# Tiles of 384 rows in a ring of four, and a last store in three pieces, in a grouped softmax

## The chip, the cores and the metric

One core of a Trainium2 chip. The metric is the device time of one execution in microseconds (us). A difference under 2% counts as "same", whatever its sign, so this case is about the sign and the size inside those 2%.

Where the text speaks of single DMA packets, it means the packet records of the trace: start, length, size and queue of each packet that a DMA engine moved. They carry no engine number. A DMA of 128 partitions also leaves 16 records of 4 B (688 for the 43 loads of the changed kernel), and the three pieces of its last store leave 16, 14 and 8. I read them as one per engine that took part, left when that engine is done, and call them end records.

## The reference

```python
B, N, D, G = 4, 4096, 4352, 8          # x: float32
x_g = x.reshape(B, N, G, D // G)
x_g = x_g - x_g.max(axis=-1, keepdims=True)
exp = np.exp(x_g)
out = exp / exp.sum(axis=-1, keepdims=True)
```

16384 rows, each with eight softmaxes over 544 numbers. 285.2 MB come in and 285.2 MB go out.

## The kernel before

A tile is 256 rows, two per partition (`R = 2`), in a ring of six buffers (`NT = 6`). SyncE issues loads, VectorE takes maxima, reciprocals and scales, ScalarE takes the exponentials and issues the stores. A store trails by two tiles and is issued as soon as a new tile has been seen.

```python
R = 2; NT = 6; S = R * NT; LAG = 2
...
def vector_max(n):
    s = n % S
    if s % R == 0:
        take(nc.vector, landed[s // R], 16)
        nc.vector.sem_inc(seen, 1)
    nc.vector.reduce_max(out=mx[:, s, :], in_=row(s), axis=X, negate=True).then_inc(max_done, 1)
...
def store(b, target):
    take(nc.scalar, scaled, R)
    nc.scalar.dma_start(out=target, in_=bufs[b][:, :]).then_inc(stored[b], 16)

def scalar_tile(j, *targets):
    take(nc.scalar, seen)
    for r in range(R):
        if r < len(targets):
            store((j - LAG + r) % NT, targets[r])
        scalar_exp(j * R + r)
...
scalar_tile(nt - 2, ot[nt - 4])
scalar_tile(nt - 1, ot[nt - 3], ot[nt - 2])
store((nt - 1) % NT, ot[nt - 1])           # the last store: one DMA of 128 partitions
...
def vector_rows(lo, hi):
    for n in range(lo, hi):
        vector_max(n + 1)
        vector_scale(n)
```

## Time and profile before

| | before |
|---|---|
| median time, 3 runs | 1330.36 us (1330.23 to 1330.4) |
| span | 1328.5 us |
| VectorE busy / ScalarE busy | 1041.7 / 764.5 us |
| the two DMA queues together | 99.5% of 16 engines' span |
| last store done on 13 engines / two more / the last one | 1319.9 to 1320.3 / 1322.4 / 1326.3 us |

Read it from the bottom: the DMA engines are always busy, so only the edges of the run can be won. The lines are in the prediction. The columns are the stretch in us, its length, the busy time of VectorE, ScalarE and GpSimd (with the number of instructions), the clock, the DMA share and GB/s. A packet counts, whole, in the stretch in which it starts, so a short stretch can be off by one round of packets, and a share can pass 1.

```profile
66.00:82.00 16.00, 15.70 (x21) 11.44 (x32) 0.00 (x0) 1.00 0.97 418
82.00:100.00 18.00, 17.70 (x21) 13.44 (x38) 0.00 (x0) 1.00 1.00 433
1294.00:1309.00 15.00, 6.72 (x17) 5.55 (x16) 0.00 (x0) 1.00 1.03 446
1310.00:1319.80 9.80, 0.00 (x0) 0.00 (x0) 0.00 (x0) 1.00 0.93 401
1320.40:1326.30 5.90, 0.00 (x0) 0.00 (x0) 0.00 (x0) 1.00 0.08 35
```

The reader is to see a full rate up to 1320 and then 6 us in which one slow engine works off its lag.

### The profile page before, as it was taken

The page shows a single profiled execution, that of the slowest core. Times are in us where ns is not written, and L with a number is a line of the kernel's source. Part 1 is how long each engine was busy: PE and PEld are TensorE (multiplying, and loading weights), DVE is VectorE, ACT ScalarE, POOL GpSimd, SP SyncE. Part 2 cuts the span into 40 slices and gives each one's busy share as a digit, 9 for nine tenths or more (in the row PEclk, how much of TensorE's full clock was granted, in tenths as well). Part 3 has the DMA queues.
Part 4 walks back from the last instruction along what each step waited for, and adds up shares of the span by engine and source line. Part 5 has one row for each costly group of instructions (what it writes and reads, how often), then busy time and mean ns, then how long its engine had stood idle before and what let it go on. Part 6 is the DMA issues. An engine that isn't in the chain of part 4 may idle for free. (4 is left out here: it accounts for less than half of the span.)

```text
span 1328.5 us, 4328 instructions
## 1 busy us (share of the span) xinstructions
DVE 1041.7 (78%) x1280; ACT 764.5 (58%) x2049; POOL 0.2 (0%) x4
## 2 busy tenths in 40 slices
DVE  5899987887877878778787787877878778787781
ACT  3677755655556556565565655655556555565551
POOL 0000000000000000000000000000000000000000
DMA  9999999999999999999999999999999999999997
GB/s 403 418 436 435 434 433 429 432 435 436 435 433 428 432 435 436 435 434 430 429 436 435 435 434 433 426 436 436 434 434 433 427 435 436 435 434 433 427 433 328
DMA packets 18439, 570.49 MB, mean 429 GB/s; under 512 B 2048, under 2 KB 2048, under 8 KB 2048
## 3 DMA queue, kind: packets, MB, share of 16 engines
q1 hardware_dynamic: 9216, 285.22, 49.8%
q10 hardware_dynamic: 9216, 285.22, 49.7%
q14 instruction: 7, 0.06, 0.0%
HBM read 285.21 MB, written 285.21 MB: 429 GB/s over the span
## 5 line engine op out<-in xcount | busy, mean ns | idle before, releaser
L88 ACT ACTIVATE xt<-xt,mx 128x544 f32<-128x544 f32 x1024 | 751.3, 735 | 534.1 <-ACTq L59 534.1
L70 DVE TENSOR_REDUCE mx<-xt 128x8 f32<-128x4352 f32 x128 | 599.2, 4682 | 238.3 <-DVEq L59 235.3
L79 DVE TENSOR_SCALAR xt<-xt,rs 128x544 f32<-128x544 f32 x1024 | 434.2, 498 | 19.2
L88 ACT ACTIVATION_READ_ACCUMULATOR xt<-xt,mx 128x1 f32 x1024 | 192.0, 187 | 0.0
L75 DVE RECIPROCAL rs<-sm 128x8 f32<-128x8 f32 x128 | 24.8, 193 | 4.2 <-DVEq L59 4.2
L120 ACT ACT_TABLE_LOAD x1 | 1.3, 1283 | 0.9 <-SPq L47 0.9
L156 POOL MEMSET const-bfloat16-1.0<- 128x1 bf16 x1 | 0.1, 103 | 0.0
L156 POOL MEMSET const-uint8-127<- 128x1 uint8 x1 | 0.1, 102 | 0.0
L156 POOL MEMSET const-float32-0.0<- 128x1 f32 x1 | 0.1, 100 | 0.2 <-issue 0.2
L156 POOL MEMSET const-float32-1.0<- 128x1 f32 x1 | 0.1, 99 | 0.0
## 6 DMA issues: line engine op xcount, KB each, us to landing
xt<-in_x_dram SPq DMA_DIRECT2D x64, 4352.0 KB, 30.5
out_dram<-xt ACTq DMA_DIRECT2D x64, 4352.0 KB, 51.3
```

Source lines behind the costliest of these rows:

```text
L70: nc.vector.reduce_max(out=mx[:, s, :], in_=row(s), axis=X, negate=True).then_inc(max_done, 1)
L75: nc.vector.reciprocal(out=rs[:, s, :], in_=sm[:, s, :]).then_inc(rec_done, 1)
L79: i = nc.vector.tensor_scalar_mul(out=xr[:, g, :], in0=xr[:, g, :], scalar1=rs[:, s, g:g + 1])
L88: i = nc.scalar.activation(out=xr[:, g, :], in_=xr[:, g, :], func=Exp, bias=mx[:, s, g:g + 1], scale=1.0, accum_out=sm[:, s, g:g + 1],)
L120: nc.scalar.preload_act_table(Exp)
L156: nc = _bacc.Bacc("TRN2", target_bir_lowering=False, num_devices=1)
```

## The change

The intent: fewer and longer packets (three rows per partition in place of two), the same 12 rows in SBUF, and at the end less work for two of the engines (4 packets in place of 8), so that a slow one among them no longer ends alone. The `seen` semaphore goes: the store of tile j-1 now comes after the exponential of tile j's first row.

```diff
-    R = 2
-    NT = 6
+    R = 3
+    NT = 4
     ...
-    def scalar_tile(j, *targets):
-        take(nc.scalar, seen)
-        for r in range(R):
-            if r < len(targets):
-                store((j - LAG + r) % NT, targets[r])
-            scalar_exp(j * R + r)
+    def scalar_tile(j, target):
+        scalar_exp(j * R)
+        take(nc.scalar, scaled, R)
+        nc.scalar.dma_start(out=target, in_=tile_of(j - 1)).then_inc(stored[(j - 1) % NT], 16)
+        for n in range(j * R + 1, min((j + 1) * R, nr)):
+            scalar_exp(n)
     ...                                   # 42 tiles of 384 rows, one of 256
-    store((nt - 1) % NT, ot[nt - 1])
+    take(nc.scalar, scaled, last_rows)
+    for lo, hi in ((0, 64), (64, 120), (120, P)):
+        nc.scalar.dma_start(
+            out=ot_last[lo:hi, :], in_=tile_of(last)[lo:hi, :]).then_inc(stored[last % NT], 16)
```

More of the change, by code (lines that the diff above doesn't have):

```diff
@@ L19 @@
     P = 128
-    R = 2
-    NT = 6
+    R = 3
+    NT = 4
     S = R * NT
-    LAG = 2
     xf = x.flatten_outer_dims()
@@ L27 @@
     Dg = D // G
-    nt = N // (P * R)
-    turns = (nt - LAG) // NT
-    rest = LAG + turns * NT
-    assert rest == nt - 2
+    nr = N // P
+    last = (nr - 1) // R
+    last_rows = nr - last * R
+    nt = last + 1
+    turns = (last - 1) // NT
     f32 = mybir.dt.float32
@@ L34 @@
     Exp = mybir.ActivationFunctionType.Exp
-    xt = xf.rearrange("(t p r) d -> t p (r d)", p=P, r=R)
-    ot = of.rearrange("(t p r) d -> t p (r d)", p=P, r=R)
-    turn_out = of[:turns * S * P, :].rearrange("(u b p r) d -> u b p (r d)", b=NT, p=P, r=R)
+    xt = xf[:last * P * R, :].rearrange("(t p r) d -> t p (r d)", p=P, r=R)
+    ot = of[:last * P * R, :].rearrange("(t p r) d -> t p (r d)", p=P, r=R)
+    turn_out = of[:turns * P * S, :].rearrange("(u b p r) d -> u b p (r d)", b=NT, p=P, r=R)
+    xt_last = xf[last * P * R:, :].rearrange("(p r) d -> p (r d)", p=P)
+    ot_last = of[last * P * R:, :].rearrange("(p r) d -> p (r d)", p=P)
     landed = [tc.alloc_semaphore(f"landed{b}") for b in range(NT)]
     stored = [tc.alloc_semaphore(f"stored{b}") for b in range(NT)]
-    seen = tc.alloc_semaphore("seen")
     max_done = tc.alloc_semaphore("max_done")
@@ L59, in take, with tile_of @@
         engine.sem_inc(sem, -n).wait_op(sem, n, "sem-ge")
+    def tile_of(t):
+        return bufs[t % NT][:, :(R if t < last else last_rows) * D]
     def row(s):
@@ L68, in vector_max @@
             take(nc.vector, landed[s // R], 16)
-            nc.vector.sem_inc(seen, 1)
         nc.vector.reduce_max(out=mx[:, s, :], in_=row(s), axis=X, negate=True).then_inc(max_done, 1)
@@ L96, in scalar_exp @@
         i.then_inc(exp_done, 1)
-    def store(b, target):
+    def scalar_tile(j, target):
+        scalar_exp(j * R)
         take(nc.scalar, scaled, R)
-        nc.scalar.dma_start(out=target, in_=bufs[b][:, :]).then_inc(stored[b], 16)
-    def scalar_tile(j, *targets):
-        take(nc.scalar, seen)
-        for r in range(R):
-            if r < len(targets):
-                store((j - LAG + r) % NT, targets[r])
-            scalar_exp(j * R + r)
+        nc.scalar.dma_start(out=target, in_=tile_of(j - 1)).then_inc(stored[(j - 1) % NT], 16)
+        for n in range(j * R + 1, min((j + 1) * R, nr)):
+            scalar_exp(n)
     for t in range(nt):
@@ L114 @@
             nc.sync.wait_ge(stored[b], 16 * (t // NT))
-        nc.sync.dma_start(out=bufs[b][:, :], in_=xt[t]).then_inc(landed[b], 16)
+        nc.sync.dma_start(
+            out=tile_of(t), in_=xt[t] if t < last else xt_last).then_inc(landed[b], 16)
     for b in range(NT):
-        nc.sync.wait_ge(stored[b], 16 * ((nt - b + NT - 1) // NT))
+        parts = 2 if b == last % NT else 0
+        nc.sync.wait_ge(stored[b], 16 * ((nt - b + NT - 1) // NT + parts))
     nc.scalar.preload_act_table(Exp)
-    for j in range(LAG):
-        scalar_tile(j)
+    for n in range(R):
+        scalar_exp(n)
     with loop(nc.scalar) as u:
         for b in range(NT):
-            scalar_tile(LAG + b, turn_out[u, b])
-    scalar_tile(nt - 2, ot[nt - 4])
-    scalar_tile(nt - 1, ot[nt - 3], ot[nt - 2])
-    store((nt - 1) % NT, ot[nt - 1])
+            scalar_tile(b + 1, turn_out[u, b])
+    for j in range(turns * NT + 1, nt):
+        scalar_tile(j, ot[j - 1])
+    take(nc.scalar, scaled, last_rows)
+    for lo, hi in ((0, 64), (64, 120), (120, P)):
+        nc.scalar.dma_start(
+            out=ot_last[lo:hi, :], in_=tile_of(last)[lo:hi, :]).then_inc(stored[last % NT], 16)
     def vector_rows(lo, hi):
@@ L136 @@
     vector_max(0)
-    vector_rows(0, LAG * R)
+    vector_rows(0, R)
     with loop(nc.vector):
-        vector_rows(LAG * R, LAG * R + S)
-    vector_rows(rest * R, nt * R - 1)
-    vector_scale(nt * R - 1)
+        vector_rows(R, R + S)
+    vector_rows(R + turns * S, nr - 1)
+    vector_scale(nr - 1)
 _INS = ['x']
```

## The prediction

> **What bounds the kernel now.** I read, in this order: the page's bars by slice and DMA rows (which resource is full), the issues with their times to landing, the DMA queue's own waits, the engines' groups, and last the timeline where the loads end.
>
> ```profile
> DVE 1041.7 (78%) x1280; ACT 764.5 (58%) x2049; POOL 0.2 (0%) x4
> ...
> DMA  9999999999999999999999999999999999999997
> GB/s 403 418 436 435 434 433 429 432 435 436 435 433 428 432 435 436 435 434 430 429 436 435 435 434 433 426 436 436 434 434 433 427 435 436 435 434 433 427 433 328
> DMA packets 18439, 570.49 MB, mean 429 GB/s; under 512 B 2048, under 2 KB 2048, under 8 KB 2048
> ...
> q1 hardware_dynamic: 9216, 285.22, 49.8%
> q10 hardware_dynamic: 9216, 285.22, 49.7%
> ...
> xt<-in_x_dram SPq DMA_DIRECT2D x64, 4352.0 KB, 30.5
> out_dram<-xt ACTq DMA_DIRECT2D x64, 4352.0 KB, 51.3
> ```
>
> The two DMA queues together fill 99.5% of 16 engines for the whole span. VectorE is idle 22% of it, ScalarE 42%. So bytes bound the kernel: 570.4 MB near 434 GB/s. Three slices are lower: the first two (403, 418) and the last (328). Those edges are all that this change can win or lose; between them the rate is flat. One load takes 30.5 us to land and one store 51.3 us, although a tile's share of the time is 1328.5/64 = 20.8 us: both queues always have work waiting.
>
> ```profile
> SPq L115 <- DMA out_dram<-xt: 1225.8, 58, 73.6
> SPq L117 <- DMA out_dram<-xt: 77.2, 1, 77.2
> ```
>
> The loader waits only for stores to leave a buffer; it never makes the DMA engines wait while stores are queued.
>
> ```profile
> 48.61 5.47 ACTq L100 DMA_DIRECT2D out_dram<-xt  x1
> ...
> 56.38 4.68 DVE L70 TENSOR_REDUCE mx<-xt 128x8 f32<-128x4352 f32 x1 [3.05 <-issue]
> ...
> 63.08 0.34 ACTq L100 DMA_DIRECT2D out_dram<-xt  x1
> ```
>
> The first store is issued at 48.61, its issue takes 5.47 us (later ones 0.34), and VectorE loses 3.05 us as it enters its loop.
>
> ```profile
> 1280.54 4.69 DVE L70 TENSOR_REDUCE mx<-xt 128x8 f32<-128x4352 f32 x1 [4.08 <-DVEq L59]
> 1280.63 0.35 ACTq L100 DMA_DIRECT2D out_dram<-xt  x1
> ...
> 1288.98 0.34 ACTq L100 DMA_DIRECT2D out_dram<-xt  x1
> ...
> 1303.55 0.34 ACTq L100 DMA_DIRECT2D out_dram<-xt  x1
> ```
>
> The last tile lands just before 1280.54, and one store goes out with it, one at 1288.98, the last at 1303.55. With the ends of stores below, the DMA engines are never empty here.
>
> The trace's single DMA packet records (start, length, size, queue; no engine number) give the rest. A row pair of 34816 B is one packet: 1.288 us long, the next starts 1.2847 us after it. With both queues full the packets alternate one by one. Each DMA ends in 16 records of 4 B, one per engine: so I can see when each engine finishes a tile. In the last store they come at 1319.8 to 1320.3 for 13 engines, 1322.4 for two, and **1326.3 for one**. That one falls back evenly, by some 0.1 us per tile; for the last load it was at 1279.8 where most were at 1273.6. The span ends at 1328.5 and the time is 1330.4, so time = last DMA record + 4.1 us.
>
> [...] 64, 56 and 8 partitions then give 16, 14 and 8 engines with 4, 4 and 1 partitions each. The trace agrees for 128 partitions: 9216 packets a queue = 64 x (128 + 16). [...] The trace shows one slow engine but not its number. [...]
>
> **The change part by part.** The arithmetic per row is unchanged, and so are the bytes and the ring (12 rows). It has four parts.
>
> (a) Fewer, longer packets. Before: 128 x 8 = 1024 packets per engine x 1.2847 = 1315.5, plus 128 end records x 6 ns = 0.8: 1316.3 us. It starts at 1.9, and 1.7 are lost at the two cold starts (first packets of about 2 us in place of 1.288, once for loads and once for stores): 1319.9, as measured. [...] 84 x 8 = 672 x 1.9247 = 1293.4; the small tile 16 x 1.2847 = 20.6; 86 end records 0.5: 1314.5. **-1.8 us.**
>
> (b) The uneven last store. [...] The end moves from 6.3 above the level to 1.3: **-5.0 us.**
>
> (c) The start. Tile 0 lands after 8 x 1.925 + 1.9 + 0.9 = 18.2 us (before: 13.3). Per row VectorE needs 4.6 + 0.35 + 3.3 = 8.25 us, as the rows of the timeline are spaced. Max of row 0 runs 18.9 to 23.5, its exp to 29.5, scale to 33.5; row 1's scale ends at 41.7, max of row 3 at 46.3, its exp at 52.4. Store 0 then goes out at 52.5 and its first packet, as before 9.3 us later, at 61.8. The loads alone last to about 64.4, so nothing is empty yet. Loads, store 0 and its cold start end at 1.9 + 0.9 + 61.6 + 15.4 + 1.0 = 80.8. Store 1 needs three more rows and the exp of row 6: with the 5.5 us of the first issue and the 3 us loop entry, issue at 80 to 81.5, first packet 1.3 later. Load 4 waits for store 0 on its slowest engine and starts about 83. A hole of 0.5 to 2.5: **+1.5 us.**
>
> (d) The end. The new order stores tile j-1 only after the exp of the first row of tile j. At the last tile that is landing L + 0.7 (semaphore) + 4.6 (max) + 6.1 (exp) + 1.4 (issue to packet) = L + 12.8 us; before, a store went out with the landing itself. Without a hole the level would end at 1314.5 + 1.9 + 1.7 + 1.5 = 1319.6, and stores 41 and 42 are 15.4 + 10.3 of it: all else is moved at 1293.9. When is L? Before, loads held 30.5 of about 124 us of a buffer's round, 3 of 12 rows, and 9 rows were left to store when they ended: (1320 - 1273.6)/5.14 = 9.0. The last ring holds 11 rows, so 8 are left: 8 x 5.14 = 41 us before 1319.6, 1278.5 on most engines; the slow one is 4.2 (if it loses per packet) to 6.3 (per byte) later. L = 1283 to 1285, store 41's packets 1295.5 to 1297.6, a hole of 1.6 to 3.7: **+2.7 us.** The slow engine has no hole, which only hides part of its own lag.
>
> Sum: -1.8 - 5.0 + 1.5 + 2.7 = -2.6 us, against 1330.4: **1328.0 us**, -0.2%.
>
> **The rivals.** *The ring starves in every turn.* Store j-1 waits for tile j, and there are only 4 buffers. If each tile lost 1 us, 42 us would be added, 1372. Against: a round is 4 x 30.8 = 123 us and needs load 30.8, landing 0.7, next landing plus max and exp 43, issue 1.3, store 30.8, release and new load 1.9: 108.5. Slack 14.7 us per round, more than the 6 us lag. VectorE needs 24.8 us per tile of 30.8. *All the gain goes to the end.* If one row more is on its way in when loads end, L comes 5 us later and the hole is 7 to 8: 1332 to 1333. For: the balance is set in the first 100 us, which I can't know to a row. [...] Then it keeps its lag and perhaps a ninth packet: level + 4.2 to 7.6, 1328 to 1332; the two 2 us late ones show that lags differ. *The intent comes true without holes:* 1323.6. *Longer packets move at another rate:* 1% would be 13 us; [...] nothing seen speaks for loss.
>
> **Range and chances.** Holes of 0 to 4 at the start and 0 to 7 at the end, and the balance of (b) by 2 either way, give 1324 to 1332. 2% are 26.6 us, four times everything at stake at the edges: faster 0.5%, slower 1.5% (starving ring, longer packets), within 98%.
>
> **What would show each step.** (a) In the DMA view 6192 packets on the load queue and 6214 on the store queue (43 x 16 end records, the last store 16+14+8), the mid-span rate still 433 to 436 GB/s. (b) The last end records lie within about 3 us of each other for the engines with 8 and 9 packets, the slow one among or before them. (c) First store issue near 52.5, second near 81, a slice with a slight dip there. (d) Second-to-last store 11 to 12 us after the last landing, and a drop in the DMA share just then, near 1295. The prediction is wrong if the flat part dips in every tile, if the DMA issues show landings near 16 us (an empty partner queue), or if one engine still ends 6 us alone.

## The result, and the profile after

| | before | changed |
|---|---|---|
| median of 4 runs | 1330.3 us | 1344.42 us |
| lowest to highest | 1329.79 to 1330.4 | 1342.36 to 1352.57 |
| span of the profiled run | 1328.5 us | 1343.3 us |

The ratio is 1.0118, with a 95% interval of 1.0076 to 1.016. Here and below a ratio is the mean time of one kernel's fast runs over that of the other's in the same rounds, so it is not quite the ratio of the medians. That counts as "same" by the 2% line, but the interval is clear of 1: the changed kernel is slower, by 14 us, and 1344.4 lies outside the predicted 1324 to 1332.

From the page of the changed kernel, the rows of rate and packets:

```profile
GB/s 407 412 418 431 434 432 435 432 439 432 428 440 429 437 429 440 431 435 435 428 440 428 439 431 439 432 429 439 429 439 429 440 429 439 432 428 440 428 367 206
DMA packets 12413, 570.49 MB, mean 425 GB/s; under 512 B 1398, under 2 KB 1398, under 8 KB 1398
q10 hardware_dynamic: 6214, 285.22, 49.9%
q1 hardware_dynamic: 6192, 285.22, 49.3%
```

The flat part is as flat as before, the packet counts are the predicted 6192 and 6214, and both queues still look full, 99.2% together. The loss stands in the last two slices, 367 and 206 GB/s. That the queues are "busy" there while the rate is half is what has to be explained. The stretches around the end, same columns as above:

```profile
66.00:82.00 16.00, 15.70 (x21) 11.51 (x31) 0.00 (x0) 1.00 0.99 428
82.00:100.00 18.00, 17.70 (x21) 12.34 (x34) 0.00 (x0) 1.00 0.99 389
1284.00:1294.00 10.00, 8.83 (x11) 5.96 (x16) 0.00 (x0) 1.00 0.99 427
1294.50:1300.00 5.50, 5.35 (x11) 4.50 (x13) 0.00 (x0) 1.00 0.07 28
1300.00:1313.00 13.00, 10.12 (x18) 7.43 (x21) 0.00 (x0) 1.00 1.03 446
1315.50:1326.10 10.60, 0.00 (x0) 0.00 (x0) 0.00 (x0) 1.00 0.97 200
1326.60:1336.50 9.90, 0.00 (x0) 0.00 (x0) 0.00 (x0) 1.00 0.68 155
```

Two different things are to be seen. From 1294.5 to 1300.0 the engines are **empty** (share 0.07). From 1315.5 to 1326.1 they are **full and slow**: share 0.97, but 200 GB/s where the kernel before moved 401 in its last store. The packet records say the same of single packets: in the first piece the 64 packets are 2.3 to 3.0 us long, half of them 2.71, for 34816 B that took 1.288 us almost everywhere in the kernel before. The last store as a whole takes from 1315.5 to 1341.6, 26.1 us in place of 8 x 1.288 = 10.3.

The timeline at the last landing (start, length, engine, line, operation):

```profile
1290.69 4.69 DVE L73 TENSOR_REDUCE mx<-xt 128x8 f32<-128x4352 f32 x1 [1.02 <-DVEq L60]
1295.29 0.19 DVE L78 RECIPROCAL rs<-sm 128x8 f32<-128x8 f32 x1
1295.63 3.39 DVE L82 TENSOR_SCALAR xt<-xt,rs 128x544 f32<-128x544 f32 x8
...
1299.14 0.35 ACTq L105 DMA_DIRECT2D out_dram<-xt  x1
...
1313.72 3.53 ACTq L132 DMA_DIRECT2D out_dram<-xt  x3
```

The max at 1290.69 is that of the last tile's first row; behind it stands the scale of the last row of the tile before, and only then can that tile's store go out, at 1299.14. The three pieces take 3.53 us to issue in sum (0.56, 0.88 and 2.04), but the first is out at 1313.72, ahead of the 1315.5 at which the engines are ready for it.

### The profile page after: what moved, and what is told of

Read it like the earlier page. It is cut to its first block, busy times and chain, and to the rows that moved or that the text cites.

```text
span 1343.3 us, 4077 instructions
## 1 busy us (share of the span) xinstructions
DVE 1040.3 (77%) x1280; ACT 764.4 (57%) x2049; POOL 0.2 (0%) x4
## 3 DMA queue, kind: packets, MB, share of 16 engines
q10 hardware_dynamic: 6214, 285.22, 49.9%
q1 hardware_dynamic: 6192, 285.22, 49.3%
## 5 line engine op out<-in xcount | busy, mean ns | idle before, releaser
L121 ACT ACT_TABLE_LOAD x1 | 1.3, 1283 | 0.9 <-SPq L48 0.9
```

The source lines that it names most:

```text
L121: nc.scalar.preload_act_table(Exp)
```

## The experiments

Two theories for the last store were open. **Place**: how long a packet takes depends on the partitions that its DMA covers. A piece within 0 to 63 or within 64 to 127 takes about 2.7 us per packet, as in the first piece of the changed kernel; one that lies as much below partition 64 as above it takes 1.29, as the whole store of the kernel before. That a piece of 32 to 95 would do so too was the estimate; why the partitions matter, no run shows. **Pieces**: every DMA has a cost of its own (issue, first packet, end), or the second and third piece use too few engines (14 and 8). Where an expectation below gives figures for several theories, those of place come first. The diffs leave out the count in the final wait, which follows the number of pieces.

### e1 and e10: the last store whole

```diff
-    for lo, hi in ((0, 64), (64, 120), (120, P)):
+    for lo, hi in ((0, 128),):
```

> The changed kernel with its last store as one DMA of 128 partitions. In the changed kernel all engines finish the store before at 1315.5 us and the last store takes until 1341.6, 26.1 us for 8 packets per engine. Both theories of the pieces [...] expect 8 x 1.288 = 10.3 us here, an end at 1325.9 and a time of about 1329.5. If the loss lay in the longer tiles and not in the pieces, the time would stay near 1344.

> The changed kernel with its last store whole, again. [...] 26.1 - 10.3 = 15.8 us less for the last store, and as the slow engine then ends last by up to 2 us, 12 to 15 us below the changed kernel of the same call; three runs before gave 1328, 1332 and 1336.

The first time four runs gave 1328.1 to 1336.4, median 1334.0 (ratio to the kernel before 1.002, interval 0.9987 to 1.0054). The spread was too wide for a price, so the changed kernel was run again with the last store whole (e10) and in pieces (e9). They were run on another chip. Whole: median 1330.0 of 22 runs (1327.9 to 1339.9), ratio to before 1.0006, interval 0.999 to 1.0021. The kernel before lay between 1329.4 and 1331.0 in 26 of its 27 runs, and once at 1346.9.

### e9: the changed kernel again

> The changed kernel again, beside the next run on the same chip, to price the pieces: 1342 to 1352 as before. The spread of 10 us seen over its first four runs either belongs to the pieces, then the next run has less, or to the longer tiles, then it has as much.

1345.24 us median of four (1344.5 to 1348.7). So the pieces cost 1345.2 - 1330.0 = **15.2 us**, against 15.8 that the last store itself took longer. The spread does not belong to the pieces: the whole store has as much of it.

From the profile of e10, the stretches of the hole and of the last store:

```profile
1293.50:1299.00 5.50, 5.35 (x11) 4.34 (x12) 0.00 (x0) 1.00 0.07 28
1314.80:1324.80 10.00, 0.00 (x0) 0.00 (x0) 0.00 (x0) 1.00 0.91 390
```

The hole is still there, and the last store runs at full rate (its 128 packets take 1.29 to 1.30 us each). With it whole, the changed kernel is as fast as the one before, no more.

### e2: two halves

```diff
-    for lo, hi in ((0, 64), (64, 120), (120, P)):
+    for lo, hi in ((0, 64), (64, 128)):
```

> The changed kernel with its last store as two DMAs, partitions 0-63 and 64-127, both on 16 engines. [...] packets of 2.7 us, 8 x 2.7 = 21.7 us, time about 1341. Theory of too few engines (14 and 8 in the second and third piece): all 16 work here, so about 10.4 us and 1329.5. Theory of a cost per piece (three pieces cost 15.7): two thirds of it or less, 1335 to 1340, with packets of 1.29 us.

1339.5 us median (1338.3 to 1341.6). All 16 engines take part in both halves, and most packets are 2.71 us long; the last store runs from 1316.9 to 1338.1, 21.2 us against 21.7 expected by place.

```profile
1317.00:1327.50 10.50, 0.00 (x0) 0.00 (x0) 0.00 (x0) 1.00 0.80 162
1328.00:1337.50 9.50, 0.00 (x0) 0.00 (x0) 0.00 (x0) 1.00 0.84 176
```

Both stretches open just after 16 packets have started and so understate the rate: 4.46 MB in 21.2 us are 210 GB/s, against 433 for the 10.3 us of a whole store. Too few engines falls as the main cause: no engine is left out here, and the rate is still half.

### e3: three pieces, the first across the middle

```diff
-    for lo, hi in ((0, 64), (64, 120), (120, P)):
+    for lo, hi in ((32, 96), (0, 32), (96, 128)):
```

> The changed kernel with its last store as three DMAs, partitions 32-95, 0-31, 96-127. [...] its 4 packets take 1.29 us each (5.2 us); the other two have 2 packets per engine at 2.7 us (5.4 us each): 16 us, time about 1335. Theory of a cost per piece: three pieces as in the changed kernel, time about 1344 and no packet length that depends on the place. Theory of too few engines: all on 16, 1329.5.

1333.8 us median (1333.6 to 1339.1).

```profile
1314.80:1319.80 5.00, 0.00 (x0) 0.00 (x0) 0.00 (x0) 1.00 0.80 341
1320.20:1325.20 5.00, 0.00 (x0) 0.00 (x0) 0.00 (x0) 1.00 0.57 111
1325.50:1329.20 3.70, 0.00 (x0) 0.00 (x0) 0.00 (x0) 1.00 0.66 151
```

(These stretches are short; compare the rows with each other.) The piece of partitions 32 to 95 has packets of 1.29 us (a few up to 1.56) and is done in some 5.3 us; the piece of partitions 0 to 63 took 10.8 in the changed kernel. The two have the same queue, the same size, the same 16 engines and the same place in the order: only the partitions differ. In the pieces 0 to 31 and 96 to 127 of the same run the packets take 2.2 to 3.0 and 1.3 to 2.7 us. Together 15.6 us, 16 expected. The theory of place holds in these runs, and a cost per piece of the needed size does not. One rival is left here: with the partitions, the rows of `out_dram` that they go to change as well. e4 answers it.

### e4: the pieces in the kernel before

```diff
-    store((nt - 1) % NT, ot[nt - 1])
+    take(nc.scalar, scaled, R)
+    for lo, hi in ((0, 64), (64, 120), (120, P)):
+        nc.scalar.dma_start(...)
```

> The kernel before with only its last store cut into the three pieces 64, 56 and 8. [...] about 26 us instead of 10.3 for the last store, starting at the 1309.7 us at which most engines end the store before: 1336 to 1339 for the last record, time 1340 to 1343. If the pieces did what they are meant to do and the loss lay in the tiles of 384 rows, the time would be 1325 to 1330.

1335.6 us median (1335.0 to 1336.0), ratio 1.0035, interval 1.0018 to 1.0052.

```profile
1310.00:1319.80 9.80, 0.00 (x0) 0.00 (x0) 0.00 (x0) 1.00 1.05 274
1320.00:1332.00 12.00, 0.00 (x0) 0.00 (x0) 0.00 (x0) 1.00 0.47 165
```

Slower than before, as place expects, but by 5.4 us and not by 10 to 13. The packet records show why: here no hole has lined the engines up. They come to the last store up to 11 us apart, so some are already in the second piece (partitions 64 to 119) while others are in the first, and many packets take 1.288 us again. Two pieces in one queue do overlap when their engines are out of step. The same pieces, to the same partitions and the same rows of `out_dram`, that took 2.7 us per packet in the changed kernel take 1.29 here on several engines; so neither the rows of `out_dram` nor the partitions alone make a packet slow; I read it as an effect of what the other engines are doing at that moment.

The records of this run settle another point. The slow engine can be followed by its late packets: after its part of the store before it takes 4, then 4, then 1 packet. It is in all three pieces, so it is one of the eight engines of the third (the records show how many engines a piece uses, 16, 14 and 8, but not which). Most of the 5.4 us can be followed on this engine, which ends the run: while the others were already in the first piece, the last four packets of its store before took 9.5 us in place of 5.2, and its ninth packet adds 1.3.

### e6: which engine is slow

```diff
-    for lo, hi in ((0, 64), (64, 120), (120, P)):
+    for lo, hi in ((0, 64), (64, 120), (120, 127), (127, P)):
```

> The kernel before with its last store in pieces of 64, 56, 7 and 1 partitions[...]. In the run with 64, 56 and 8 the slow engine took part in all three pieces[...]. Time about 1335, as with three pieces.

1336.1 us in a single run (its state is unknown). The chain of late packets again has 4, 4 and 1 packets, so the slow engine takes part in the piece of seven partitions, as it did in that of eight, and is not one of the two with four packets. Two chains come within 10 ns of each other at one place, and I followed the one that gives each its eight packets of the store before. By this the change hands its slow engine nine packets, the largest share. (e4 and e6 ran on two different chips; that the slow engine is the same one on both, and in the changed kernel, is assumed.)

### e5: without the wait for the last tile

The whole last store, and at the last tile the scale and the store of the tile before ahead of the max that waits for the load.

```diff
-    for j in range(turns * NT + 1, nt):
+    for j in range(turns * NT + 1, last):
         scalar_tile(j, ot[j - 1])
+    take(nc.scalar, scaled, R)
+    nc.scalar.dma_start(out=ot[last - 1], in_=tile_of(last - 1)).then_inc(stored[(last - 1) % NT], 16)
+    for n in range(last * R, nr):
+        scalar_exp(n)
     ...
-    vector_rows(R + turns * S, nr - 1)
+    vector_rows(R + turns * S, last * R - 1)
+    vector_scale(last * R - 1)
+    vector_max(last * R)
+    vector_rows(last * R, nr - 1)
```

> The changed kernel with its last store whole, and at the last tile the scale and the store of the tile before placed ahead of the max that waits for the last load. The hole of about 6 to 8 us in most DMA engines between the stores of tiles 40 and 41 goes. Theory that the hole costs its length: 6 to 8 us less than with the whole last store alone (1334.0), about 1327. Theory that the one slow engine hides it (it ended store 40 at 1302.7, when the others had waited until 1301): the slow engine sets the end alone, at 1302.7 + 15.4 + 10.3 = 1328.5, so 0 to 2 us less, 1332 to 1334, with one end record 5 to 9 us after the others.

1330.7 us median (1330.5 to 1332.6), ratio to before 1.0004, interval 0.9991 to 1.0017: neither of the two figures. It was run on another chip. In its timeline:

```profile
1291.55 0.20 DVE L78 RECIPROCAL rs<-sm 128x8 f32<-128x8 f32 x1 [2.58 <-DVEq L60]
...
1295.40 0.35 ACTq L130 DMA_DIRECT2D out_dram<-xt  x1
...
1315.83 0.34 ACTq L136 DMA_DIRECT2D out_dram<-xt  x1
```

The store of tile 41 goes out at 1295.40 in place of 1298 to 1300, while fifteen engines run out between 1294.3 and 1296.4. But the last store goes out at 1315.83, and most engines had ended the one before at 1311.7 to 1311.9: the hole has moved, to 5 us before the last store. VectorE had no slack to give: after tile 41 it has five rows of about 8.25 us each to do, and the new order makes it wait 2.58 us for an exponential on the way. So I read the hole as the time of the arithmetic of the last two tiles, not as the place of one wait; no run made that arithmetic shorter to test it.

### e7: the short tile first

The tile of 256 rows is tile 0, then come 42 tiles of 384; the order at the end as in e5. One line of a longer edit, which renumbers rows and tiles:

```diff
-    return bufs[t % NT][:, :(R if t < last else last_rows) * D]
+    return bufs[t % NT][:, :(R if t else F) * D]          # F = 2
```

> As the kernel without the hole, but the tile of 256 rows comes first instead of last, so the first store can start about 7 us earlier and the DMA engines do not run empty near 81 us. Theory that the start hole costs its length (1.5 us by the rate of the slice from 66 to 100 us): 1 to 3 us less than the kernel without the hole. Theory that only the slow engine and the end count: no difference. The last store is now 384 rows, which may open a hole of up to 5 us on most engines at the end, behind the slow one.

1340.9 us median (1332.1 to 1341.7), ratio 1.0067: a miss. The first store did go out earlier (37.6 us), but the last tile is now three rows of arithmetic, and its store went out at 1320.2 when most engines had ended the one before at 1306.7. Fifteen of the 16 engines stood still for 13 to 14 us where I had allowed 5 (the slow one, done at 1317.2, for 4). One engine was up to 23 us behind in this run, far more than in any other; I don't know why. The run says nothing of a hole at the start: the packet records show none there to remove (see (c) below).

### e8: four short tiles at the end

40 tiles of 384 rows, then four of 256, each store whole. Some lines of a longer edit, shortened:

```diff
-    last = (nr - 1) // R
+    short = 4                       # of Q = 2 rows
+    long = (nr - Q * short) // R
```

> 40 tiles of 384 rows and the last four of 256, every last store whole, otherwise the changed kernel's order. Theory that the hole near the end comes from the size of the last tiles (a tile's store waits for a whole next tile to land): with short tiles the last load lands earlier against the stores left, the hole of 6 to 8 us is gone or under 2, most engines end near 1320, the slow one 5 to 7 later: time 1328 to 1331, at or just below the kernel before. Rival, that the order of the new loop makes it (store after the next tile's first max): the hole stays at 5 us or more and the time is 1332 to 1336.

1343.5 us median (1337.0 to 1345.3), ratio 1.009: a miss too. Three engines fell 12 us behind over the last tiles; the last load landed on them at 1304 (on the others by 1292 to 1297), and holes opened before both of the last stores. The rival (the hole stays, the time is 1332 to 1336) was nearer but is not shown by this either: the time lies above it. What makes engines fall behind at some tile sequences stays open.

No version beat the kernel before by more than the noise; the changed one with its last store whole (1330.0) and e5 (1330.7) equal it.

## Why the prediction was wrong

**What bounds the kernel** was right: the flat part kept its rate and only the edges moved.

**(a) Longer packets: right.** In the packet records a tile of 384 rows takes 30.807 us in the flat part, and one and a half of the old tiles 1.5 x 20.5675 = 30.851. The difference times 42.7 tiles is 1.9 us; 1.8 was predicted. The 1.9247 us from packet to packet that the prediction counts with was the estimate; the trace gives (30.807 - 2 x 0.006)/16 = 1.9247.

**(b) The uneven last store: the step that failed.** It was to gain 5.0 us: a slow engine with 4 packets in place of 8 would have 4 x 1.285 = 5.1 us less, and those with 4+4+1 = 9 would end last, 1.3 us after the level. Against a whole store it costs 15.2. The term that failed is the price of a packet: I counted packets per engine and gave each 1.285 us, wherever its partitions lie, and in the pieces most took 2.7. Only the number of engines was asked for, not the partitions of each piece. The runs show what these did: 2.7 us per packet in 0 to 63 and in 64 to 127 (e2), 1.29 in 32 to 95 (e3). The last piece is worse still: of the eight packets from partitions 120 to 127, one took 1.29 us and the others 1.7 to 4.9, and the piece was done 4.8 us after the second one.

Two more assumptions of (b) fell. The slow engine is not one of the two with four packets (e4, e6), a rival that the prediction named ("it keeps its lag and perhaps a ninth packet"). And there was no lag left to remove: the hole of (d) let the slow engine, done at 1299.8, catch up with the others, which waited until 1300.1 for packets. All 16 ended the store before the last within 0.3 us of each other.

**(c) The start: the size was right, the reason was not.** A hole worth 1.5 us was predicted. From 82 to 100 us the rate is 389 in place of 433 GB/s, 18 x 44/433 = 1.8 us lost; from 66 to 82 it is 428 in place of 418, 0.4 gained: 1.4. But the DMA share there is 0.99: no hole. By the packet records each engine stood empty for less than 0.1 us between 70 and 86 us. Instead some thirty packets took 2.0 to 3.9 us in place of 1.93 as the loads came back, from 86 to 94 us. In the profiles of e1, e2, e3 and e10, with the same order at the start, this costs 0.2 us or less per engine, in e5 and e9 1.7 and 1.4. So the agreement is luck; why the packets are slow in some runs stays open. The first two stores went out at 50.9 and 80.2, for 52.5 and "80 to 81.5".

**(d) The end: the hole and its place were right, its size and part of its path were not.** A hole of 2.7 us was predicted near 1295. Fifteen engines ran out between 1294.4 and 1296.4 and had packets again at 1300.0 to 1300.1: up to 5.7 us, 4.8 on average. The level at which it starts was right to 0.5 us (1293.9). The last landing was at 1290.1 and not at 1283 to 1285: the loads were one to two rows further behind than assumed, and the slow engine 7 us late. One ingredient was wrong in the other direction: the exponential is not on the path. ScalarE's sequencer issued the store at 1299.14, in the middle of it. The path is landing, max, reciprocal and scale: 9.0 us from landing to issue and some 10 to the first packet (0.9 after the issue, for the assumed 1.4), not 12.8. The rival "one row more, hole of 7 to 8" was the nearer one. e5 adds that the wait I blamed is not the whole of it: without it the hole moved, and VectorE's work on the last two tiles is the likely root.

**The sum.** For the engines that run out first: they ended at 1319.9 in the kernel before; -1.9 (a), +1.4 (c) and +5.7 (d) give 1325.1, and 26.1 - 10.3 = 15.8 for the pieces 1340.9; measured 1341.6. In e10's profile (c) cost next to nothing and the hole was 6.4 us (1292.8 to 1299.2): 1319.9 - 1.9 + 6.4 = 1324.4; measured 1325.1. Both come out 0.7 us short. (The prediction's own sum has a slip: 1330.4 - 2.6 is 1327.8, not 1328.0.) Without (b), its gain of 5.0 goes too: the prediction would have been 1330.4 - 1.8 + 1.5 + 2.7 = 1332.8, against the 1330.0 of the whole store. The slow engine's lag of 6.3 us did go away there, but through the hole and not through the pieces.

## What to carry to other kernels

When a transfer is cut by partitions, look at the packet length of each cut and not only at how many engines it gets; a cut across the middle (32 to 95) kept 1.29 us per packet where 0 to 63, on 16 engines too, took 2.71. A DMA share near 1.0 says that engines are occupied, not that they move bytes at full rate (0.97 went with 200 GB/s here, 0.93 with 401): read it together with GB/s. And before evening out a lag among engines, look whether anything ahead of that point has already let the slow one catch up.

## What else was measured

- Two transfers of disjoint partitions in one queue followed each other when the engines were in step (21.2 us, e2), less so when they were up to 11 us apart (e4 lost 5.4 us for three pieces).
- The slow engine, with DMAs from SyncE and ScalarE, took part in the piece of eight partitions (e4) and, by my reading of one trace, in that of seven (e6). In the kernel before it lost some 0.1 us per tile of 20.6 us.
- The first store of the kernel before took 5.47 us to issue (2.18 in the changed kernel), later ones 0.34; the three pieces took 0.56, 0.88 and 2.04.
- How far single engines fall behind differed between the sequences of tiles tried here: 5 to 7 us in most profiles, up to 23 in e7; the cause was not found.
